# A hybrid decoder layer on one core: the output projection over all 512 tokens of a quarter, norm 2's row scales behind the up projection, and a triangular inverse in place

## The chip, the core and the metric

The kernel runs on one core of a Trainium2 chip. The metric is the device time of one execution in microseconds, the median of several runs; lower is better. The engines are TensorE (PE; PEld is its weight load), VectorE (DVE), ScalarE (ACT), GpSimd (POOL) and SyncE (SP, which issues most of the DMAs).

## The reference

One step of one layer over 2048 prompt tokens and 8 single-token samples, all in float32. Two mixers run side by side on the normed input, a diagonal state space (S5, 512 channels) and a gated delta net (4 heads of 128). Then comes what the change is about:

```python
n = rmsnorm(x, norm1_g); proj = n @ w_in                       # 1024 -> 2568
y_s5 = s5_mixer(...); y_gdn = gdn_mixer(...)                   # chunks of the delta net solve (I + L) X = R, L strictly lower triangular
x = x + concat(y_s5, y_gdn) @ w_out                            # 1024 -> 1024
h = rmsnorm(x, norm2_g) @ w_up                                 # 1024 -> 5632
h = causal_depthwise_conv(h, width 3); gate, up = split(h)
x = x + (silu(gate) * up) @ w_down                             # 2816 -> 1024
y = rmsnorm(x, normf_g)
```

## The kernel before

Activations lie transposed, channels on partitions and tokens in columns. The tokens are worked through in four quarters of 512 (`QT`); the first carries the 8 samples behind its tokens (`NQ` = 520 columns). Each product is made to float32 accuracy out of three matmuls of rounded operands: both sides are split into `hi` and `lo` (`split`: a rounding copy on ACT, a subtraction on DVE or POOL), and `mm3` (L286) adds hi x hi, hi x lo and lo x hi in PSUM. A weight tile is 128 output channels by 1024 inputs. `wsplit` loads it into one of `NWR` = 2 raw buffers `wr` and splits it into `whi` and `wlo`, of which there are four pairs (`NW` = 8). `mm24` (L305) runs its 24 matmuls, 8 input tiles by 3. PSUM tiles hold 512 columns; the tags `mm` (projections) and `d` (down projection) have two each. `blocks(q)` are one block of 512 columns, or 256 and 264 in the first quarter; `halves(q)` are two halves in all quarters.

Program order comes from strings of letters (`FFN`, L44): `r` is the next piece of the generator `rest()`, F, I and B are the front, the inverse and the back of a delta net head, so that a quarter's FFN runs beside the next quarters' heads. A scheduler then sets each engine's order from that and from its estimate of times; what it made of the change is shown further below.

Quarters count from 0 in the code. For a quarter q, `ffn` (L1203) does this:

- `ffn_mix` (L1113, called at the end of the quarter before) loads the mixers' outputs and splits them into `nT`.
- `ffn_out` (L1134) runs over the first half of the tokens, then over the second, each over 8 tiles of `w_out`, which so are loaded and split twice. L1144 adds the product to the residual `xr`, loaded by `ffn_res` for two channel tiles and a half of the tokens, into `x2`. `add_squares` (L1101) sums the squares on ACT and POOL.
- Norm 2: `ffn_scales` (L1150) sums over channels with a matmul with ones and takes the inverse root. `ffn_norm` applies weights and row scales to the first half (L195, then a split, L71 and L72) while the second half's projection runs. For the second half only the channels' weights go into `nT` (L1233, L1234); its row scales `rs` come at L1250.
- Four tiles of w_up (`UPS`) are run ahead, in quarters 1 to 3: their first halves before the second half's norm is done, the second halves after it.
- In a loop over 11 pairs of channel tiles, the up projection leaves PSUM through L1249 (ACT, first half) and L1250 (DVE, second half, times `rs`); then come the convolution (L1251, L1254), the gate and the split into `gt`, and `ffn_down` (L1083) adds w_down's product into `x2` at L1097.
- The last `ffn_down` goes over the halves, with squares (L1105, L1107) and the final weights (L1176) behind each group. `finish` (L1178) takes the root of the squares (a matmul with ones, L1185), transposes `x2` (L1196) and writes the result times the row scale (L1198). Its second half is called as `fin` inside the next quarter's `ffn_out`, after its tile 1.

`gdn_inverse` (L890) makes the inverse of I - L for the four chunks of a head out of `LT`, in the tile `T2T`, of which there are two.

Of the kernel before, what the change touches and what calls it, by code (L numbers as in the profile page):

```python
# [1453 lines left out]
```

## Time and profile before

| | us |
|---|---|
| runs of the kernel | 2874.18, 2874.52, 2877.04 |
| their median | 2874.52 |
| span of the profiled execution, first to last instruction | 2874.3 |
| PE busy in it | 2715.0 (94%) |
| DVE busy | 2176.9 (76%) |
| ACT busy | 1476.0 (51%) |
| POOL busy | 609.6 (21%) |
| HBM read and written | 279.29 MB and 47.29 MB |

The profiled execution's own time is its span, and it stands at the runs' median. Busy is the time in which at least one instruction of the engine runs. Matmuls overlap, so a busy PE isn't yet one at its peak; how close it is shows in the distance between starts. The granted clock is the share of PE's full 2.4 GHz that it was given; half of it is 1.2 GHz.

### The profile page before, as it was taken

What the parts mean: (1) busy time and instruction counts of PE and PEld (TensorE: products, weight loads), DVE (VectorE), ACT (ScalarE), POOL (GpSimd) and SP (SyncE); (2) the same over time, 40 slices, a digit from 0 to 9 for tenths busy, and PEclk for the clock granted to TensorE, in tenths of its full rate; (3) what the DMA queues carried; (4) which work ended last, traced back from release to release, by engine and by line L of the source; (5) the groups of instructions that cost most, each with busy time, mean ns of one, the idle gap of its engine ahead of it and who ended that gap; (6) DMA issues with size and microseconds to landing.
All of it is one profiled execution on the core that took longest, in us unless ns stands there. A gap on an engine that the chain in (4) does not pass through costs nothing.

```text
span 2874.3 us, 45554 instructions
## 1 busy us (share of the span) xinstructions
PE 2715.0 (94%) x16103; PEld 2337.9 (81%) x16103; DVE 2176.9 (76%) x4964; ACT 1476.0 (51%) x3051; POOL 609.6 (21%) x970
## 2 busy tenths in 40 slices
PE   6998788899999999998899999999999998999998
PEld 4798676786888999998887888878888787888887
DVE  8949898856688787778588687887768667676666
ACT  4446565653665554455564554555545445444444
POOL 4325332100121122222221100113211112211112
PEclk9999887898999999999999999999999999999999
DMA  7644433453644232233533333245333334523332
GB/s 205 199 134 132 113 109 92 105 133 104 182 110 117 77 103 87 89 97 111 155 115 109 100 91 98 84 137 174 93 96 97 90 93 144 157 88 96 95 97 74
DMA packets 457657, 329.30 MB, mean 115 GB/s; under 512 B 74960, under 2 KB 412249, under 8 KB 457412
## 3 DMA queue, kind: packets, MB, share of 16 engines
q1 hardware_dynamic: 447091, 297.77, 35.8%
q0 software_dynamic: 10336, 28.61, 3.4%
q8 instruction: 127, 2.08, 0.3%
q14 instruction: 103, 0.84, 0.1%
HBM read 279.29 MB, written 47.29 MB: 114 GB/s over the span
## 4 chain that ended last, share of the span: by engine, by line
PE 66%; DVE 17%; DMA 8%; ACT 4%; issue 3%; POOL 0%; SPq 0%; DVEq 0%; POOLq 0%; ACTq 0%
PE psmm L287 15%; PE psmm L288 15%; PE psmm L289 15%; PE psd L287 5%; PE psd L288 5%; PE psd L289 5%; DVE wlo L72 3%; DVE t L823 1%; ACT whi L71 1%; DVE X L907 1%; DMA xr<-xTD 1%; DMA mr<-mixT 1%; DVE x L1097 1%; DVE hh L649 1%; DMA wr<-in_w_out_dram 1%
## 5 line engine op out<-in xcount | busy, mean ns | idle before, releaser
L287 PE MATMUL psmm<-nT,whi 128*128 128x512 f32 (+2 forms) x3232 | 1115.5, 347 | 45.2 <-ACT whi L71 9.6
L288 PE MATMUL psmm<-nT,whi 128*128 128x512 f32 (+2 forms) x3232 | 1110.3, 344 | 4.8 <-DVE nT L224 3.0
L289 PE MATMUL psmm<-nT,wlo 128*128 128x512 f32 (+2 forms) x3232 | 1107.2, 343 | 1.7 <-POOL wlo L72 1.0
L287 PEld LDWEIGHTS psmm<-nT,whi 128*128 128x128 f32 x3232 | 622.5, 193 | 120.3 <-ACT whi L71 11.7
L288 PEld LDWEIGHTS psmm<-nT,whi 128*128 128x128 f32 x3232 | 624.5, 193 | 73.1 <-DVE nT L224 4.5
L71 ACT ACTIVATE whi<-wr 128x1024 fp32r<-128x1024 f32 x404 | 427.2, 1059 | 496.3 <-PE psmm L288 309.9
L289 PEld LDWEIGHTS psmm<-nT,wlo 128*128 128x128 f32 x3232 | 623.0, 193 | 72.4 <-issue 1.9
L72 DVE TENSOR_TENSOR wlo<-wr,whi 128x1024 fp32r<-128x1024 f32 x388 | 482.3, 1246 | 193.2 <-ACT whi L71 187.4
L1097 DVE TENSOR_TENSOR x<-psd,x 128x512 f32<-128x512 f32 (+2 forms) x464 | 255.6, 558 | 127.3 <-PE psd L289 125.2
L287 PE MATMUL psd<-gt,whi 128*128 128x512 f32 (+2 forms) x928 | 323.6, 350 | 12.7 <-DVE x L1097 10.4
L288 PE MATMUL psd<-gt,whi 128*128 128x512 f32 (+2 forms) x928 | 316.5, 342 | 0.0
L289 PE MATMUL psd<-gt,wlo 128*128 128x512 f32 (+2 forms) x928 | 314.6, 340 | 0.0
L1254 DVE SCALAR_TENSOR_TENSOR t<-raw,cc,t 128x512 f32<-128x512 f32 x352 | 271.5, 772 | 37.1 <-ACT t L1251 27.5
L1255 POOL COPY halo<-raw 128x2 f32<-128x2 f32 x176 | 49.6, 282 | 850.7 <-DVE raw L1250 765.9
L1251 ACT ACTIVATE t<-raw,cc 128x512 f32<-128x512 f32 (+1 forms) x176 | 127.2, 723 | 170.0 <-DVE raw L1250 156.7
L287 PEld LDWEIGHTS psd<-gt,whi 128*128 128x128 f32 x928 | 175.0, 189 | 42.5 <-DVE x L1097 18.8
L72 POOL TENSOR_TENSOR gt<-s,gt 128x512 fp32r<-128x512 f32 (+1 forms) x88 | 134.7, 1531 | 350.4 <-ACT gt L71 341.6
L288 PEld LDWEIGHTS psd<-gt,whi 128*128 128x128 f32 x928 | 175.1, 189 | 20.6
L289 PEld LDWEIGHTS psd<-gt,wlo 128*128 128x128 f32 x928 | 174.9, 189 | 20.8
L1107 POOL TENSOR_TENSOR sq<-sq 128x256 f32<-128x256 f32 (+1 forms) x112 | 109.8, 981 | 219.1 <-ACT sq L1105 213.1
L906 DVE TENSOR_TENSOR tm<-X,N 128x124 f32<-128x124 f32 (+30 forms) x496 | 125.4, 253 | 26.7 <-DMA N<-nD 17.6
L907 DVE TENSOR_TENSOR X<-X,tm 128x124 f32<-128x124 f32 (+30 forms) x496 | 129.6, 261 | 8.4
(503 smaller groups left out, 3666.5 us busy)
## 6 DMA issues: line engine op xcount, KB each, us to landing
wr<-in_ffn_w_up_dram SPq DMA_DIRECT2D x176, 512.0 KB
wr<-in_ffn_w_down_dram SPq DMA_DIRECT2D x88, 512.0 KB
wr<-in_w_in_dram SPq DMA_DIRECT2D x64, 512.0 KB
wr<-in_w_out_dram SPq DMA_DIRECT2D x64, 512.0 KB
xTD<-xT SPq DMA_DIRECT2D x32, 256.0 KB
N<-nD SPq DMA_DIRECT2D x16, 512.0 KB
mr<-mixT SPq DMA_DIRECT2D x32, 256.0 KB
xr<-xTD SPq DMA_DIRECT2D x32, 256.0 KB
```

What stands on the lines that cost most here:

```text
L71: nc.scalar.activation(hi, raw, AF.Copy)
L72: (eng or nc.vector).tensor_tensor(lo, raw, f32(hi), op=OP.subtract)
L287: nc.tensor.matmul(out, lhsT=wh, rhs=xh, start=first, stop=False)
L288: nc.tensor.matmul(out, lhsT=wh, rhs=xl, start=False, stop=False)
L289: nc.tensor.matmul(out, lhsT=wl, rhs=xh, start=False, stop=last)
L906: nc.vector.tensor_tensor(m, X[:, :, j:j + 1].to_broadcast(sh), N[:, j:j + 1, j + 1:].to_broadcast(sh), op=OP.mult)
L907: nc.vector.tensor_tensor(X[:, :, j + 1:], X[:, :, j + 1:], m, op=OP.add)
L1097: nc.vector.tensor_tensor(x2[:, j, b0:b1], p, x2[:, j, b0:b1], op=OP.add)
L1107: c.nc.gpsimd.tensor_tensor(acc[0], acc[0], s, op=OP.add)
L1251: nc.scalar.activation(t[:, :n], raw[:, 2:2 + n], AF.Copy, scale=w[2])
L1254: nc.vector.scalar_tensor_tensor(t[:, :QT], raw[:, j:j + QT], w[j], t[:, :QT], op0=OP.mult, op1=OP.add)
L1255: nc.gpsimd.tensor_copy(c.halo[:, ch], raw[:, QT:QT + 2])
```

## The change

The output projection takes all 512 tokens (520 in the first quarter) per tile of w_out, so each tile is loaded and split once a quarter. In quarters 1 to 3 the first two products are made before `fin` is called and their residuals are added behind it. Only the channels' weights go into `nT` for all columns, in place, tile 0 to 6 behind the matmuls of the last product; norm 2's row scales for all tokens (`rs2`, now 520 columns) are made after the first up tile (`AT`) and multiplied in where the up projection leaves PSUM, on DVE alone. The four up tiles ahead run over 512 columns. The residual comes a channel tile at a time. The inverse is built in `LT` itself; the two `T2T` tiles are gone, and the general pool has 9 buffers for 8 (`NV`).

```diff
-    nc, gp, tt = c.nc, c.gp, c.TT
+    nc, gp, tt, T = c.nc, c.gp, c.TT, LT
...
-def ffn_out(c, q, x2, nT, b0, b1, acc, xrs):
-    nc = c.nc
-    w = b1 - b0
-    for j in range(8):
-        if j % 2 == 0:
-            xr = xrs.pop(0) if xrs else ffn_res(c, q, b0, b1, j)
-        p = c.ps("mm")[:, :w]
-        mm24(c, p, wcols(c, c.w_out, j * 128), nT, b0, b1)
-        nc.vector.tensor_tensor(x2[:, j, b0:b1], p, xr[:, j % 2], op=OP.add)
-        add_squares(c, acc, x2[:, j, b0:b1])
-        yield j
+def ffn_out(c, q, x2, nT, acc, xrs, fin):
+    nc, n = c.nc, ncols(q)
+    def product(j):
+        return j, xrs.pop(0) if xrs else ffn_res(c, q, j), proj(c, q, nT, c.w_out, j * 128)
+    def residual(j, xr, pr):
+        for b0, b1, p in pr:
+            nc.vector.tensor_tensor(x2[:, j, b0:b1], p, xr[:, b0:b1], op=OP.add)
+        add_squares(c, acc, x2[:, j, :n])
+    def columns(kt):
+        g, x, hi, lo = c.col1(C_G2 + kt), x2[:, kt, :n], nT[:, kt, 0, :n], nT[:, kt, 1, :n]
+        nc.scalar.activation(hi, x, AF.Copy, scale=g)
+        nc.vector.scalar_tensor_tensor(lo, x, g, f32(hi), op0=OP.mult, op1=OP.subtract)
+    if q:
+        first = [product(j) for j in (0, 1)]
+        fin()
+        for f in first:
+            residual(*f)
+        yield
+    for j in range(2 if q else 0, 7):
+        residual(*product(j))
+        if j % 2:
+            yield
+    last = product(7)
+    for kt in range(7):
+        columns(kt)
+    residual(*last)
+    columns(7)
...
-def ffn_norm(c, x2, nT, b0, b1, acc):
-    rsB = ffn_scales(c, acc, b1 - b0)
-    for kt in range(8):
-        norm_split(c, nT, kt, x2[:, kt, b0:b1], c.col1(C_G2 + kt), rsB, b0, b1)
-        yield
...
+    yield from ffn_out(c, q, x2, nT, acc, xrs, fin)
     ups = {}
-    if q:
-        for ch in UPS:
-            w, p = wcols(c, c.w_up, ch * 128), c.ps("mm" if len(ups) < 2 else "d")
-            mm24(c, p[:, 0:256], w, nT, *A)
-            ups[ch] = w, p
...
+    for i, ch in enumerate(UPS):
+        if i == AT:
+            rsB = ffn_scales(c, q, acc, fb.tile([128, NQ], F32, name="rs2", bufs=1))
+        if q:
+            ups[ch] = [(0, QT, c.ps("mm" if i < 2 else "d"))]
+            mm24(c, ups[ch][0][2], wcols(c, c.w_up, ch * 128), nT, 0, QT)
...
-                ps = [ups[ch][1]] if ch in ups else [p for _, _, p in proj(c, q, nT, c.w_up, ch * 128)]
-                nc.scalar.activation(raw[:, 2:2 + b0], ps[0][:, :b0], AF.Copy)
-                nc.vector.tensor_tensor(raw[:, 2 + b0:2 + b1], ps[-1][:, -(b1 - b0):], rsB, op=OP.mult)
+                for b0, b1, p in ups.get(ch) or proj(c, q, nT, c.w_up, ch * 128):
+                    nc.vector.tensor_tensor(raw[:, 2 + b0:2 + b1], p, rsB[:, b0:b1], op=OP.mult)
```

The scheduler's order at three places. First PE, where the third quarter ends and the fourth's output projection goes on; before the change (`psd` holds the down projection's groups and the transposes, `psmm` the projections; `x_6015` is `x2`, `nT_6016` is `nT`):

```order
L289 MATMUL psd<-gt,wlo 128x256
L1196 MATMUL psd<-ident,x_6015 128x128 x12
L1185 MATMUL psf<-ones,sq 128x1 x2
L287 MATMUL psmm<-nT_6016,whi 128x256
L288 MATMUL psmm<-nT_6016,whi 128x256
L289 MATMUL psmm<-nT_6016,wlo 128x256
...
L1196 MATMUL psd<-ident,x_6015 128x128 x4
L287 MATMUL psmm<-nT_6016,whi 128x256
L1196 MATMUL psd<-ident,x_6015 128x128 x4
```

and now (`x2` is `x_6011`, the lines are those of the changed file, L1194 for L1185, L1205 for L1196, L285 to L287 for L287 to L289):

```order
L287 MATMUL psd<-gt,wlo 128x256
L1205 MATMUL psd<-ident,x_6011 128x128 x12
L1194 MATMUL psf<-ones,sq 128x1 x2
L1205 MATMUL psd<-ident,x_6011 128x128 x20
L285 MATMUL psmm<-nT_6012,whi 128x512
```

The 20 transposes of the last group of four and of the second half stood between matmuls of the projection, four at a time; now they stand in one piece ahead of it, and the first two products' 48 matmuls stand further up, between the groups of the down projection.

Second, DVE at the end of the fourth quarter's output projection, before (L1144 adds the residual, L195 and the L72 on `nrm` are the first half's norm, L1234 the second half's, L72 on `wr` splits a weight tile):

```order
L1144 TENSOR_TENSOR x_6015<-psmm,xr 128x256
L195 SCALAR_TENSOR_TENSOR nrm<-x_6015,cc,rq 128x256
L72 TENSOR_TENSOR wlo<-wr,whi 128x1024
L1234 SCALAR_TENSOR_TENSOR nT_6016<-x_6015,cc,nT_6016 128x256 x3
L1144 TENSOR_TENSOR x_6015<-psmm,xr 128x256
L1234 SCALAR_TENSOR_TENSOR nT_6016<-x_6015,cc,nT_6016 128x256
L72 TENSOR_TENSOR nT_6016<-nrm,nT_6016 128x256
L1234 SCALAR_TENSOR_TENSOR nT_6016<-x_6015,cc,nT_6016 128x256 x2
L195 SCALAR_TENSOR_TENSOR nrm<-x_6015,cc,rq 128x256 x2
```

and now (L1141 adds the residual, L1147 is the norm, L1172 begins the row scales):

```order
L1141 TENSOR_TENSOR x_6011<-psmm,xr 128x512
L72 TENSOR_TENSOR wlo<-wr,whi 128x1024
L1147 SCALAR_TENSOR_TENSOR nT_6012<-x_6011,cc,nT_6012 128x512 x6
L1141 TENSOR_TENSOR x_6011<-psmm,xr 128x512
L1147 SCALAR_TENSOR_TENSOR nT_6012<-x_6011,cc,nT_6012 128x512
L72 TENSOR_TENSOR wlo<-wr,whi 128x1024
L1147 SCALAR_TENSOR_TENSOR nT_6012<-x_6011,cc,nT_6012 128x512
L1172 TENSOR_SCALAR rq<-psf,epscol 128x512
```

Two chains of norm work over halves have become one over all tokens, with the last residual inside it and the row scales behind it.

Third, DVE inside the first quarter's FFN, before (L1250 is the second block's eviction; the first block's is L1249 on ACT; L906 and L907 are a head's inverse):

```order
L1250 TENSOR_TENSOR raw<-psmm,rs_8677 128x264
L907 TENSOR_TENSOR X<-X,tm 128x4x10
L1097 TENSOR_TENSOR x_6015<-psd,x_6015 128x256
L906 TENSOR_TENSOR tm<-X,N 128x4x9
L1097 TENSOR_TENSOR x_6015<-psd,x_6015 128x256
```

and now (L1238 evicts both blocks):

```order
L1238 TENSOR_TENSOR raw<-psmm,rs_8562 128x264
L1095 TENSOR_TENSOR x_6011<-psd,x_6011 128x256
...
L1095 TENSOR_TENSOR x_6011<-psd,x_6011 128x256
L904 TENSOR_TENSOR tm<-X,N 128x4x10
L1238 TENSOR_TENSOR raw<-psmm,rs_8562 128x256
```

The first block's eviction, ACT's before, stands in DVE's queue between the other work.

## Rows read from the trace of the kernel before

**Rows 1.** The page, part 1 (busy us, share of the span, instructions) and part 4.

```profile
PE 2715.0 (94%) x16103; PEld 2337.9 (81%) x16103; DVE 2176.9 (76%) x4964; ACT 1476.0 (51%) x3051; POOL 609.6 (21%) x970
...
PE 66%; DVE 17%; DMA 8%; ACT 4%; issue 3%; POOL 0%; SPq 0%; DVEq 0%; POOLq 0%; ACTq 0%
```

**Rows 2.** Stretches: length, busy us of PE, PEld, DVE, ACT, POOL, clock, DMA.

```profile
720.00:840.00 120.00, 109.88 (x693) 99.39 (x692) 93.33 (x213) 73.62 (x167) 22.64 (x29) 0.96 0.56 158
840.00:1310.00 470.00, 466.87 (x3678) 445.39 (x3677) 370.64 (x877) 242.69 (x487) 107.65 (x209) 1.00 0.33 93
1310.00:1475.00 165.00, 148.52 (x1089) 136.99 (x1088) 117.80 (x264) 90.54 (x198) 37.74 (x52) 0.96 0.47 137
1475.00:1915.00 440.00, 437.10 (x2125) 350.08 (x2123) 353.55 (x764) 232.14 (x454) 58.11 (x123) 1.00 0.34 99
1915.00:2030.00 115.00, 107.74 (x824) 102.75 (x823) 88.53 (x186) 64.46 (x138) 34.57 (x41) 0.97 0.54 162
2395.00:2505.00 110.00, 95.84 (x698) 90.06 (x697) 76.33 (x135) 52.47 (x96) 35.04 (x38) 0.94 0.53 158
```

**Rows 3.** Timeline of PE: start us, us, instruction, idle us before it and releaser.

```profile
792.67 0.56 PE L287 MATMUL psmm<-nT,whi 128*128 128x264 f32 x1 [5.70 <-ACT ot L958]
1411.24 0.47 PE L287 MATMUL psmm<-nT,whi 128*128 128x512 f32 x1 [3.07 <-ACT whi L71]
2451.27 0.58 PE L287 MATMUL psmm<-nT,whi 128*128 128x256 f32 x1 [3.20 <-DVE x L1144]
2474.56 0.55 PE L287 MATMUL psmm<-nT,whi 128*128 128x256 f32 x1 [3.02 <-ACT whi L71]
```

**Rows 4.** The chain of waits before three of these gaps: start us, us, what.

```profile
784.36 6.82 DMA wr<-in_w_out_dram
...
2444.45 6.33 DMA xr<-xTD
...
2462.06 4.67 DMA wr<-in_w_out_dram
```

**Rows 5.** Groups by line and shape: count | busy us, mean ns | idle before.

```profile
L72 DVE TENSOR_TENSOR wlo<-wr,whi 128x1024 fp32r<-128x1024 f32 x388 | 482.3, 1246 | 193.2 <-ACT whi L71 187.4 <-DMA out_dram<-S0s 1.8 <-PE psd L287 0.9
L71 ACT ACTIVATE whi<-wr 128x1024 fp32r<-128x1024 f32 x404 | 427.2, 1059 | 496.3 <-PE psmm L288 309.9 <-DMA wr<-in_ffn_w_up_dram 58.4 <-DMA wr<-in_w_out_dram 33.4
L1097 DVE TENSOR_TENSOR x<-psd,x 128x512 f32<-128x512 f32 x240 | 163.1, 686 | 95.6 <-PE psd L289 93.8
L1250 DVE TENSOR_TENSOR raw<-psmm,rs 128x256 f32<-128x256 f32 x126 | 52.6, 417 | 0.0
```

**Rows 6.** Timeline of PE behind the gap that ends at 2451.27.

```profile
2451.65 0.42 PE L288 MATMUL psmm<-nT,whi 128*128 128x256 f32 x1
...
2456.78 0.41 PE L288 MATMUL psmm<-nT,whi 128*128 128x256 f32 x1
```

**Rows 7.** Timeline of PE at full clock, pairs in succession.

```profile
2438.36 0.28 PE L289 MATMUL psmm<-nT,wlo 128*128 128x256 f32 x1
2438.47 0.28 PE L287 MATMUL psmm<-nT,whi 128*128 128x256 f32 x1
...
2600.16 0.39 PE L287 MATMUL psd<-gt,whi 128*128 128x512 f32 x1
2600.39 0.39 PE L288 MATMUL psd<-gt,whi 128*128 128x512 f32 x1
```

**Rows 8.** Stretches in which a quarter's last down projection runs.

```profile
1915.00:1954.00 39.00, 35.23 (x243) 30.95 (x241) 37.50 (x83) 24.48 (x54) 13.32 (x17) 1.00 0.47 140
2395.00:2432.00 37.00, 29.52 (x192) 24.68 (x190) 32.75 (x61) 19.11 (x36) 13.33 (x15) 1.00 0.45 141
```

**Rows 9.** Timeline of PE: transposes after the third quarter, and at the kernel's end.

```profile
2428.71 0.66 PE L1196 MATMUL psd<-ident,x 128*128 128x128 f32 x4
...
2432.78 0.39 PE L287 MATMUL psmm<-nT,whi 128*128 128x256 f32 x1
...
2861.51 0.65 PE L1196 MATMUL psd<-ident,x 128*128 128x128 f32 x4 [0.16 <-DVE x L1097]
...
2867.66 1.24 PE L1196 MATMUL psd<-ident,x 128*128 128x128 f32 x8 [1.03 <-ACT yout L1198]
```

More of the change, by code (lines that the diff above doesn't have):

```diff
@@ L23 @@
 NCH = 256
-NW, NWR, NV, NG, NM, UPB = 8, 2, 8, 4, 9, 1
+NW, NWR, NV, NG, NM, UPB = 8, 2, 9, 4, 9, 1
 PB = dict(mm=2, f=2, b=1, i=1)
-UPS = (0, NCT, 1, NCT + 1)
-FIN = 1
 NP = 0
 SMP = 0
+UPS = (0, NCT, 1, NCT + 1)
+AT = 1
 UNQ = (3, 2, 1)
@@ L150, in consts @@
     nc.gpsimd.memset(c.halo, 0.0)
-    c.T2 = [cp.tile([128, 4, 128], F32, name=f"T2T{i}") for i in range(2)]
     c.TT = cp.tile([128, 4, 64], F32, name="TT")
-    for t in (*c.T2, c.TT):
-        nc.gpsimd.memset(t, 0.0)
+    nc.gpsimd.memset(c.TT, 0.0)
     c.Xi = cp.tile([128, 4, 32], F32, name="Xi")
@@ L942, in gdn_inverse, with gdn_back @@
     nc.scalar.activation(T[0:64, :, 64:128], px3[0:64], AF.Copy)
-def gdn_back(c, q, h, col, F, T):
+def gdn_back(c, q, h, col, F):
     nc, gp, sm = c.nc, c.gp, c.sm
     S0 = c.Sst[:, h]
-    kq, kg, vt, AT, hc, zs, _ = F
+    kq, kg, vt, AT, hc, zs, T = F
     ot = gp.tile([128, QT], F32, name="ot", bufs=1).rearrange("p (a b) -> p a b", a=4)
@@ L1120, in ffn_mix @@
         split(nc, nT[:, k, 0, :n], nT[:, k, 1, :n], raw[:, :n])
-    return [ffn_res(c, q, *halves(q)[0], j) for j in (0, 2)]
-def ffn_res(c, q, b0, b1, j):
-    w, e = b1 - b0, min(b1, QT)
-    kp = lambda t: t.rearrange("(k p) t -> p k t", p=128)
-    xr = c.V("xr")[:, :2 * w].rearrange("p (k t) -> p k t", k=2)
-    c.nc.sync.dma_start(xr[:, :, :e - b0], kp(c.xTD)[:, j:j + 2, q * QT + b0:q * QT + e])
-    if b1 > QT:
-        c.nc.sync.dma_start(xr[:, :, e - b0:], kp(c.xTD)[:, j:j + 2, 2048:2056])
-    return xr
@@ L1135, in ffn_out @@
-def ffn_out(c, q, x2, nT, b0, b1, acc, xrs):
-    nc = c.nc
-    w = b1 - b0
-    for j in range(8):
-        if j % 2 == 0:
-            xr = xrs.pop(0) if xrs else ffn_res(c, q, b0, b1, j)
-        p = c.ps("mm")[:, :w]
-        mm24(c, p, wcols(c, c.w_out, j * 128), nT, b0, b1)
-        nc.vector.tensor_tensor(x2[:, j, b0:b1], p, xr[:, j % 2], op=OP.add)
-        add_squares(c, acc, x2[:, j, b0:b1])
-        yield j
-def ffn_scales(c, acc, w, y=None):
-    nc = c.nc
-    a, t = (c.V("rq")[:, :w] for _ in range(2))
-    y = c.V("rq")[:, :w] if y is None else y
-    p = c.ps("f")[:, :w]
-    nc.tensor.matmul(p, lhsT=c.ones, rhs=acc[0], start=True, stop=True)
-    nc.vector.tensor_scalar(a, p, 1.0 / D, c.epscol, op0=OP.mult, op1=OP.add)
-    return rsqrt_(nc, a, y, t)
@@ L1160, in ffn_norm, with ffn_res @@
-def ffn_norm(c, x2, nT, b0, b1, acc):
-    rsB = ffn_scales(c, acc, b1 - b0)
-    for kt in range(8):
-        norm_split(c, nT, kt, x2[:, kt, b0:b1], c.col1(C_G2 + kt), rsB, b0, b1)
-        yield
+    return [ffn_res(c, q, j) for j in (0, 1)]
+def ffn_res(c, q, j):
+    xr = c.V("xr")
+    c.nc.sync.dma_start(xr[:, :QT], c.xTD[j * 128:(j + 1) * 128, q * QT:(q + 1) * QT])
+    if q == 0:
+        c.nc.sync.dma_start(xr[:, QT:NQ], c.xTD[j * 128:(j + 1) * 128, 2048:2056])
+    return xr
+def ffn_out(c, q, x2, nT, acc, xrs, fin):
[25 more added lines that the diff above has]
+    columns(7)
@@ L1168, in ffn_final, with ffn_scales @@
+def ffn_scales(c, q, acc, y):
+    nc = c.nc
+    for b0, b1 in blocks(q):
+        a, t = (c.V("rq")[:, :b1 - b0] for _ in range(2))
+        p = c.ps("f")[:, :b1 - b0]
+        nc.tensor.matmul(p, lhsT=c.ones, rhs=acc[0][:, b0:b1], start=True, stop=True)
+        nc.vector.tensor_scalar(a, p, 1.0 / D, c.epscol, op0=OP.mult, op1=OP.add)
+        rsqrt_(nc, a, y[:, b0:b1], t)
+    return y
 def ffn_final(c, q, x2):
@@ L1207, in ffn @@
     A, B = halves(q)
[L1208 to L1237 removed]
+    acc = []
+    yield from ffn_out(c, q, x2, nT, acc, xrs, fin)
+    ups = {}
+    for i, ch in enumerate(UPS):
[4 more added lines that the diff above has]
+            mm24(c, ups[ch][0][2], wcols(c, c.w_up, ch * 128), nT, 0, QT)
     yield
@@ L1342, in step @@
                 q, h, col, F = st.todo.pop(0)
-                gdn_back(c, q, h, col, F, c.T2[h % 2])
+                gdn_back(c, q, h, col, F)
             elif s == "N":
```

27 lines of the change are left out of this document (2 added, 25 removed).

## The prediction

> **What bounds the kernel now.** (The code counts quarters from 0; first to fourth are its 0 to 3.) I read the page's busy line first: TensorE (PE) is busy for 2715.0 of 2874.3 us, VectorE (DVE) for 2176.9, ScalarE (ACT) for 1476.0 [rows 1]. A share over the whole span says little here, so I cut the FFN part of the span into stretches [rows 2]. Inside a quarter's FFN PE stands idle for 3.1 us in 470 and 2.9 in 440: nothing but PE matters there. Between two quarters, where the output projection and norm 2 lie, it idles 10.1 of 120 us, 16.5 of 165, 7.3 of 115 and 14.2 of 110, together 48.1 us, and there its granted clock is 0.96, 0.96, 0.97 and 0.94 of full, where the FFN stretches show 1.00. One minus the clock, times the length, is 4.8 + 6.6 + 3.5 + 6.6 = 21.5 us at most. So about 70 us lie in the four transitions, and a change of the projection and of norm 2 can win no more than that plus what PE's own work shrinks.
>
> Then I looked for what ends PE's idle time there. Four of the longest rows are 5.70, 3.07, 3.20 and 3.02 us [rows 3]. The chain of waits names what came last before them [rows 4]: a load of a tile of w_out (6.82 us), a residual load (6.33 us, queued behind weight loads), and not long before the fourth another load of w_out (4.67 us), between the whi (1.06 us) and wlo (1.25 us) of other tiles [rows 5]. That loop explains the stretch. There are two raw weight buffers, and one is free again when whi and wlo are made of it, so a tile takes (4.67 + 1.06 + 1.25) / 2 = 3.5 us at least while the loads take that long. PE asks for a tile every 24 x 0.12 = 2.9 us when the tile meets 256 columns. It starves by some 0.6 us a tile, and the start of the stage, where several loads crowd, makes long gaps of it.
>
> After such a gap PE runs slowly: behind the one of 3.20 us 25 matmuls of 256 columns follow each other, the first at 2451.65, the last at 2456.78, 0.21 us apart [rows 6], where 0.12 is the pace at full clock [rows 7]: 25 x 0.09 = 2.3, with the first one 2.5 us more.
>
> **The change part by part.**
>
> Fewer, longer matmuls. In quarters 1 to 3, 8 tiles of w_out and 4 of w_up go from two matmuls of 256 columns to one of 512: 3 x 12 x 24 = 864 pairs. At full clock a row of 256 is followed after 0.11 to 0.12 us, one of 512 after 0.23 [rows 7], so the pair costs what the long one costs, to 0.01 us: I take 864 x 0.003 = 2.6 us won (9 lost to 9 won).
>
> Half the w_out tiles. 32 loads of 512 KB go, with 32 whi on ACT (1.06 us) and 32 wlo on DVE (1.25 us) [rows 5]. Those engines had slack there, so their 34 and 40 us aren't the gain. The gain is that a tile now feeds 24 x 0.233 = 5.6 us of PE against the loop's 3.5 us: the starvation ends. I credit the four long gaps, 15.0 us, with a slow stretch of 2.5 us behind each: 25 us. Upper bound: all 70 us; lower bound: 9 us, the two gaps (5.70 and 3.20) whose chain leads to w_out's own queue, without the slow stretches.
>
> More to do while the last down projection runs. That part, done in two halves with squares and scaling, is bound by DVE: 37.50 us busy of 39 at the third quarter's start, 32.75 of 37 at the fourth's [rows 8], while PE idles 3.8 and 7.5 us. The two products whose PSUM is free then are now 11.2 us of PE instead of 5.7. In the order of the third and fourth quarters they stand between the down projection's groups, in the second they come mostly after it. I take 3 us in two quarters, 6 in all (0 to 11).
>
> A wait that is new: the residual of channel tile 0 is now written over all 512 tokens, so it must follow the transposes of the last quarter's second half, and product 2 needs its PSUM. Now these transposes stand singly between matmuls; in the changed order all 20 stand in one piece, right before product 2. The kernel's own end has the same order without cover and prices it [rows 9]: from the first transpose (2861.51) to the end of the last (2868.90) 7.4 us. Of these 32 x 0.11 = 3.5 us are work that stays. Today the first 12 transposes and what follows take 4.1 us (2428.71 to 2432.78), and 20 more between matmuls some 2.2 to 2.8 us: 6.6. So 0.8 us is lost, and a slow stretch of 2.5 us comes with it, and the residual itself 0.69 us: 4 us in each of two quarters, 8 in all (2 to 13). The second quarter has 43 of the 48 matmuls behind the transposes as cover.
>
> Norm 2. Before, the first half's columns took two DVE operations and a copy each; now all take one copy and one DVE operation over 512 columns, in place, each behind the last product's matmul that reads it. Eight at about 0.75 us are 6 us beside 5.6 us of product 7 and 22 us of the four up tiles that follow; the row scales (five DVE and two ACT operations of some 0.7 us, 5 us) are asked for only by the eviction of the first up tile, 17 us of matmuls later. I cost it at 0. If the cover were gone it would be 5 us a quarter, 20 us. In quarter 0, which has no up tiles ahead, the projections of the next delta net head stand there in the order: 42 + 54 matmuls of 512 columns, 22 us.
>
> Evictions of the up projection. Today ACT takes 256 columns and DVE the rest (0.417 us); now DVE takes all, in quarters 1 to 3 as one of 512 (0.686 us, by the down projection's addition of the same shape) [rows 5]. DVE gains 132 x 0.27 = 36 us and in quarter 0, with its two blocks, 44 x 0.42 = 18 us. Inside the FFN that makes DVE 353.6 + 12 of 440 us busy in the second quarter and 370.6 + 18 of 470 in the first [rows 2], 83% each. In quarter 0 a block of matmuls lasts 24 x 0.12 = 2.9 us and two blocks of PSUM are all there is, and every block must now come through DVE's queue, behind a wlo of 1.25 us, say. I take 3 us there, 0 elsewhere (0 to 37, below).
>
> The inverse in place of L^T. No instruction goes but two memsets on POOL; L^T's buffer is held until the head's back part, as A^T's already is, and the front of the next head but one comes after that in the order. 0, and the room goes to a ninth buffer of the general pool. The stretch before 720 us is only reordered by the scheduler: 0, give or take 5 us, which no row prices.
>
> Sum: 25 + 6 + 2.6 - 8 - 3 = 23 us, from 2874.3 us of the profiled execution to **2851 us**. The median of the runs, 2874.52, is the same within 0.01%.
>
> **Rivals.**
>
> Larger gain: the transitions close nearly, 40 to 55 us won, 2819 to 2836 us. For it: 70 us are idle or slow. Against it: the DVE-bound end of each quarter and the transposes stay. 8%.
>
> The waits move: the starvation ends, but norm 2's chain, the transposes and the residual now lie in one line per quarter. If each of four quarters loses 5 us at the row scales, the 23 us are gone: 2866 to 2880 us. For it: all tokens now wait at one point, where before one half covered the other. Against it: 17 us of cover. 16%.
>
> DVE becomes the bound inside the FFN: slower. In quarter 0 there are 88 blocks; if each waits 0.42 us for the eviction that ACT used to make beside it, 37 us are lost, and the time is 2874 - 26 + 37 = 2885 us. It decides from 0.3 us a block on. For it: DVE already has 17% of the chain [rows 1]. Against it: PE idles only 3.1 us in that stretch with DVE 79% busy, and ACT had to wait for PE there as well. The Trainium skill (Perfetto Trace Analysis, Optimizing Scalar/DVE Operations) speaks for this rival: where DVE is saturated, it says, moving some work to ScalarE may help, and the change does the reverse. By that rule the trace agrees only in so far as DVE is near 80% there. 14%.
>
> That the change doesn't do what it says can be left out: the order has 32 loads of w_out fewer.
>
> **How the numbers follow.** The forecast, 2836 to 2866 us, has 62%. A measurement of this kernel tells some 0.2%, 5.7 us, from no change: faster is below 2868.8 us, slower above 2880.3. Faster: 62 + 8 and a fifth of the 16, 73%. Same: the rest of those, 13%. Slower: 14%. The range 2822 to 2876 leaves out some 2% below and 18% above.
>
> **What would show it.** Right: PE's idle time between quarters down by 15 to 25 us with no gap of 3 us behind a whi or a w_out load; the granted clock there up; the FFN stretches as long as now. Transposes: a stretch of 7 us before the third product in the last two quarters, with a clock below full behind it. Wrong: PE idle behind the multiplication by the row scales inside quarter 0, or behind the row scales' chain; or a stretch before 720 us that has moved by more than 5 us.

## The result, and the profile after

The changed kernel takes 2849.03 us (median of 4 runs, 2843.12 to 2856.1), the kernel before in the same comparison 2875.78. The ratio is 0.9907, 95% interval 0.989 to 0.9923: faster by 27 us (22 to 32). The forecast was 2851. The profiled execution, with a span of 2841.3 us, is the quickest of the four; it lies 33.0 us under the span of before, so its stages sum to more than the medians differ.

The page of the changed kernel, part 1 and part 4, against [rows 1]:

```profile
PE 2696.8 (95%) x15233; PEld 2278.9 (80%) x15233; DVE 2151.1 (76%) x4873; ACT 1383.6 (49%) x2773; POOL 668.5 (24%) x940
...
PE 72%; DVE 16%; DMA 5%; issue 3%; ACT 3%; SPq 0%; POOL 0%; POOLq 0%; DVEq 0%; ACTq 0%
```

PE was busy 18.2 us less and yet has 72% of the chain instead of 66; DMA's share fell from 8 to 5%. The stretches that answer to [rows 2], columns as there (the cuts follow the same stages):

```profile
720.00:831.00 111.00, 103.64 (x681) 92.75 (x680) 83.45 (x189) 60.58 (x132) 17.53 (x20) 0.97 0.45 124
831.00:1308.00 477.00, 472.61 (x3697) 451.47 (x3696) 381.97 (x917) 232.46 (x455) 106.04 (x211) 1.00 0.33 93
1308.00:1462.00 154.00, 144.75 (x808) 120.79 (x806) 103.77 (x227) 78.63 (x170) 35.83 (x42) 0.98 0.43 126
1462.00:1894.00 432.00, 426.84 (x2062) 341.84 (x2063) 358.44 (x764) 219.34 (x409) 82.76 (x125) 1.00 0.34 97
1894.00:2002.00 108.00, 103.50 (x544) 85.21 (x543) 71.85 (x135) 50.70 (x97) 31.61 (x33) 0.98 0.45 135
2369.00:2471.00 102.00, 93.85 (x455) 75.47 (x454) 67.31 (x111) 47.28 (x82) 32.02 (x33) 0.98 0.46 142
```

PE's idle time in the four transitions is 7.4 + 9.3 + 4.5 + 8.2 = 29.3 us, where it was 48.1. One minus the clock, times the length, is 3.3 + 3.1 + 2.2 + 2.0 = 10.6 us, where it was 21.5.

Cuts at round times don't hold the same work, so I also measured between events: a stage "FFN" runs from the first to the last addition of the down projection in a quarter (L1097 before, L1095 after), a stage "between" from that last one to the first of the next quarter. From the starts of these additions in the traces, in us:

```
                 start   FFN1  betw.1-2  FFN2  betw.2-3  FFN3  betw.3-4  FFN4
before           888.4  473.3    136.7  452.4    101.7  376.9    100.8  331.9
changed          886.8  476.4    128.6  448.8     95.2  377.7     89.2  326.4
changed-before    -1.6    3.1     -8.1   -3.6     -6.5    0.8    -11.6   -5.5
load_twice       892.1  478.9    132.8  451.1     96.3  381.5     91.3  326.4
split_twice      884.8  476.8    131.2  448.9     95.6  376.5     92.8  326.0
no_filler        886.1  466.1    140.5  441.0    104.1  371.6    102.6  326.4
spare_psum       883.6  476.9    128.5  449.2     97.5  386.4     79.9  326.7
at3              891.9  477.2    132.5  454.8     99.2  373.9     91.5  326.0
e_act_q0         890.7  480.1    128.5  449.1     96.3  377.7     89.2  326.4
t2t_after        892.9  476.5    132.3  456.4     95.4  374.4     90.7  326.5
inplace_before   886.4  474.3    148.4  446.7    106.6  377.6     98.2  331.8
inplace_nv8      898.6  475.8    137.3  450.8     99.5  378.0    101.0  331.7
nwr3_before      891.3  473.0    146.6  447.3     99.3  375.7    103.6  331.4
w_out_twice      893.6  476.6    134.1  450.4     99.8  378.0     97.1  326.0
short_mm         893.2  476.4    127.5  452.8     96.4  379.5     90.1  326.7
```

Of 33 us, 26.2 came out of the three stages between quarters, 5.5 out of the fourth FFN. That one is no faster: the trace of before has 22 more 512-column matmuls in it (886 for 864; 22 x 0.23 = 5.1 us), which the change put ahead of its first addition. The first quarter's projection lies in "start" and won next to nothing. Each row is one execution, and its sums are good to some us only: short_mm, whose runs are no longer than the changed kernel's (below), is 7.1 us longer from the first FFN on.

In the last transition the chain of waits of the changed kernel has no load from the first product after the transposes on (start us, us, what):

```profile
2388.91 4.79 DMA mixT<-zs
2393.77 2.85 DMA mr<-mixT
...
2420.28 1.24 PE psd L1205 x8
2421.52 0.38 PE psmm L285
...
2463.50 0.86 PE psf L1171 x2
```

Between the last two lines, 42 us, every piece of the chain is a matmul of PE: the loads of w_out and of the residuals, which stood there in [rows 4], are hidden. In the two transitions before it the chain has none of them either (1375 to 1462 and 1940 to 2002 us). Only the last down projection still has two transfers in the chain, the store and the load of a head's output (`mixT`).

### The profile page after: what moved, and what is told of

Same layout as the page of the kernel before. It is cut to its first block, busy times and chain, and to the rows that moved or that the text cites. A ratio compares the mean times of both kernels' runs of the same rounds, so it can differ in the third digit from the quotient of the medians.

```text
span 2841.3 us, 43162 instructions
## 1 busy us (share of the span) xinstructions
PE 2696.8 (95%) x15233; PEld 2278.9 (80%) x15233; DVE 2151.1 (76%) x4873; ACT 1383.6 (49%) x2773; POOL 668.5 (24%) x940
## 4 chain that ended last, share of the span: by engine, by line
PE 72%; DVE 16%; DMA 5%; issue 3%; ACT 3%; SPq 0%; POOL 0%; POOLq 0%; DVEq 0%; ACTq 0%
PE psmm L285 16%; PE psmm L286 16%; PE psmm L287 16%; PE psd L285 5%; PE psd L286 5%; PE psd L287 5%; DVE wlo L72 2%; DVE X L905 1%; DVE x L1095 1%; DVE tm L904 1%; DVE hh L647 1%; DVE t L821 1%; DVE nT L72 1%; DMA N<-nD 1%; DVE t L1242 1%
## 5 line engine op out<-in xcount | busy, mean ns | idle before, releaser
L285 PE MATMUL psmm<-nT,whi 128*128 128x512 f32 (+2 forms) x2992 | 1068.8, 359 | 21.3 <-ACT t L818 5.0
L286 PE MATMUL psmm<-nT,whi 128*128 128x512 f32 (+2 forms) x2992 | 1062.5, 355 | 4.7 <-DVE nT L222 3.2
L287 PE MATMUL psmm<-nT,wlo 128*128 128x512 f32 (+2 forms) x2992 | 1060.1, 355 | 1.0 <-POOL wlo L72 0.9
L71 ACT ACTIVATE whi<-wr 128x1024 fp32r<-128x1024 f32 x372 | 393.5, 1059 | 649.7 <-PE psmm L286 468.2
L285 PEld LDWEIGHTS psmm<-nT,whi 128*128 128x128 f32 x2992 | 570.4, 191 | 104.9 <-ACT t L818 7.2
L286 PEld LDWEIGHTS psmm<-nT,whi 128*128 128x128 f32 x2992 | 572.0, 191 | 83.2 <-DVE nT L222 4.8
L287 PEld LDWEIGHTS psmm<-nT,wlo 128*128 128x128 f32 x2992 | 571.1, 191 | 81.5 <-issue 2.3
L72 DVE TENSOR_TENSOR wlo<-wr,whi 128x1024 fp32r<-128x1024 f32 x356 | 439.3, 1235 | 99.6 <-ACT whi L71 94.7
L1095 DVE TENSOR_TENSOR x<-psd,x 128x512 f32<-128x512 f32 (+2 forms) x464 | 256.7, 557 | 154.3 <-PE psd L287 152.6
L285 PE MATMUL psd<-gt,whi 128*128 128x512 f32 (+2 forms) x928 | 323.7, 349 | 15.3 <-DVE x L1095 14.8
L287 PE MATMUL psd<-gt,wlo 128*128 128x512 f32 (+2 forms) x928 | 315.9, 342 | 0.0
L1242 DVE SCALAR_TENSOR_TENSOR t<-raw,cc,t 128x512 f32<-128x512 f32 x352 | 278.1, 792 | 15.7 <-ACT t L1239 11.2
L1243 POOL COPY halo<-raw 128x2 f32<-128x2 f32 x176 | 72.0, 409 | 803.1 <-DVE raw L1238 723.3
L285 PEld LDWEIGHTS psd<-gt,whi 128*128 128x128 f32 x928 | 175.4, 189 | 45.6 <-DVE x L1095 22.7
L72 POOL TENSOR_TENSOR gt<-s,gt 128x512 fp32r<-128x512 f32 (+1 forms) x88 | 130.2, 1479 | 334.0 <-ACT gt L71 333.9
L287 PEld LDWEIGHTS psd<-gt,wlo 128*128 128x128 f32 x928 | 175.3, 189 | 21.0
L1238 DVE TENSOR_TENSOR raw<-psmm,rs 128x512 f32<-128x512 f32 (+1 forms) x214 | 123.7, 578 | 69.1 <-PE psmm L287 67.6
L1105 POOL TENSOR_TENSOR sq<-sq 128x256 f32<-128x256 f32 (+3 forms) x84 | 96.4, 1148 | 207.3 <-ACT sq L1103 204.4
```

Of the source, the lines that this page charges most:

```text
L285: nc.tensor.matmul(out, lhsT=wh, rhs=xh, start=first, stop=False)
L286: nc.tensor.matmul(out, lhsT=wh, rhs=xl, start=False, stop=False)
L287: nc.tensor.matmul(out, lhsT=wl, rhs=xh, start=False, stop=last)
L1095: nc.vector.tensor_tensor(x2[:, j, b0:b1], p, x2[:, j, b0:b1], op=OP.add)
L1105: c.nc.gpsimd.tensor_tensor(acc[0], acc[0], s, op=OP.add)
L1238: nc.vector.tensor_tensor(raw[:, 2 + b0:2 + b1], p, rsB[:, b0:b1], op=OP.mult)
```

## The experiments

Intervals are those of the ratio to the kernel before, measured on the same chip. "Over the changed kernel" is the difference of the two ratios times 2876 us; by the roots of the summed squares of the intervals' halves it is good to some 6 us. So only differences of 8 us and more stand on the ratio alone; of smaller ones the stages speak. The scheduler orders each variant anew, too: 814 of PE's 15233 matmuls stand at another place than in the changed kernel in load_twice, 1663 in split_twice, 2190 in no_filler, 1426 in at3 and 2361 in e_act_q0, so no run changes one thing alone.

**w_out_twice.** Loads and splits of w_out doubled.

```diff
-        return j, xrs.pop(0) if xrs else ffn_res(c, q, j), proj(c, q, nT, c.w_out, j * 128)
...
+        p = c.ps("mm")
+        for k0 in (0, 4):
+            wh, wl = wcols(c, c.w_out, j * 128)
+            for kt in range(k0, k0 + 4):
+                mm3(nc, p, wh[:, kt], wl[:, kt], nT[:, kt, 0, :QT], nT[:, kt, 1, :QT], kt == 0, kt == 7)
+        return j, xr, [(0, QT, p)]
```

> The changed kernel, but in the second to fourth quarter each tile of w_out is loaded and split twice, once for its first four input tiles and once for the last four; the matmuls keep their 512 columns and their order. Starvation theory (the gain came from the raw buffers' loop, 3.5 us a tile): a tile is asked for every 2.8 us again, so most of the 25 us credited to it come back: 2864 to 2874 us, ratio 0.995 to 1.000, with gaps of 2 us and more on TensorE behind whi or a load of w_out between the quarters. Rival (the gain came from the longer matmuls and from more work beside the down projection; the loads were hidden): 2845 to 2854 us, ratio 0.989 to 0.993, no such gap.

Measured 2866.68 us, ratio 0.996 (0.9948 to 0.9973): 15 us over the changed kernel, as the starvation theory had it. But its gaps are not behind w_out: the longest, 7.15 us at 1476.59, is behind an eviction by the row scales. So this doesn't yet say whether transfers or splits cost it. The next two take them apart.

**load_twice** and **split_twice.**

```diff
...
+        if q:
+            c.nc.sync.dma_start(c.WR("wr").rearrange("p (k f) -> p k f", k=8),
+                                c.w_out.rearrange("(k p) f -> p k f", p=128)[:, :, j * 128:j * 128 + 128])
+        return j, xr, proj(c, q, nT, c.w_out, j * 128)
```

```diff
...
+        nc.sync.dma_start(v(wr), c.w_out.rearrange("(k p) f -> p k f", p=128)[:, :, j * 128:j * 128 + 128])
+        for k0 in (0, 4):
+            wh, wl = c.W("whi"), c.W("wlo")
+            split(nc, wh, wl, wr, c.wl)
+            for kt in range(k0, k0 + 4):
+                mm3(nc, p, v(wh)[:, kt], v(wl)[:, kt], nT[:, kt, 0, :QT], nT[:, kt, 1, :QT], kt == 0, kt == 7)
...
```

> The changed kernel with every tile of w_out in the second to fourth quarter loaded a second time into a raw buffer that nobody reads; it is split once. With the twice split twin it takes apart the kernel that did both and came out at ratio 0.996. Starvation theory (loads and raw buffers set the pace): most of that loss, 10 to 18 us over the changed kernel, 2859 to 2867 us, ratio 0.994 to 0.997. Rival (the work of splitting on ScalarE and VectorE sets it): at most 4 us over the changed kernel, ratio 0.990 to 0.992.

> The changed kernel with every tile of w_out in the second to fourth quarter loaded once but split twice, into two pairs of buffers, the first for four input tiles and the second for the other four: 24 more roundings on ScalarE (25 us) and 24 more subtractions on VectorE (30 us). Starvation theory: at most 4 us over the changed kernel, ratio 0.990 to 0.992. Rival (the splits stand in VectorE's and ScalarE's queues ahead of norm 2's columns and of the residuals): 10 to 18 us over it, ratio 0.994 to 0.997, with TensorE waiting for the columns or for the row scales.

Measured: load_twice 2858.94 us, ratio 0.9945 (0.9932 to 0.9957), 11 us over the changed kernel; split_twice 2849.15, ratio 0.9913 (0.9898 to 0.9928), 2 us. The loads cost more than the 55 us of splitting; whether the splits cost nothing can't be told. In the stages from the end of the first FFN on, load_twice is 13.5 us over the changed kernel, split_twice 5.1, which is no more than one execution can show, and w_out_twice, which does both, 19.5. The rival's wait does show in split_twice, once, at the second quarter's first eviction, as in w_out_twice:

```profile
1465.09 0.76 PE L285 MATMUL psmm<-nT,whi 128*128 128x512 f32 x1 [7.19 <-DVE raw L1249]
```

In the changed kernel this wait is 1.01 us. Where the loads cost is told by the chain of load_twice in the last transition:

```profile
2381.77 4.18 DMA wr<-in_w_out_dram
2385.97 0.38 SPq L301
2386.46 4.39 DMA mr<-mixT
...
2396.06 4.38 DMA mr<-mixT
...
2405.76 4.76 DMA mixT<-zs
2410.53 6.09 DMA mr<-mixT
```

and by SP's timeline, the queue that issues them (L1139 is the added load, L301 the one that is used, L1115 loads the mixers' outputs):

```profile
2405.09 0.38 SPq L1139 DMA_DIRECT2D wr<-in_w_out_dram  x1
...
2407.22 0.38 SPq L301 DMA_DIRECT2D wr<-in_w_out_dram  x1
2409.78 0.38 SPq L1139 DMA_DIRECT2D wr<-in_w_out_dram  x1
2410.53 0.45 SPq L1115 DMA_DIRECT2D mr<-mixT  x1
```

The first of the three pieces of the mixers' outputs stands in SP's queue behind a load of w_out, which had to wait until the added load had landed. The last piece is issued when the store that it reads has landed (2405.76 + 4.76); there it is the transfer that is long, 6.09 us where the changed kernel's chain has 2.85, with three weight loads issued in the 5.6 us before it instead of two. So the price of weight loads falls on what stands behind them, by waiting in the queue and by slower transfers; what each is worth isn't shown.

**nwr3_before.** The other side of the same question: the kernel before with a third raw buffer.

```diff
-NW, NWR, NV, NG, NM, UPB = 8, 2, 8, 4, 9, 1
+NW, NWR, NV, NG, NM, UPB = 8, 3, 8, 4, 9, 1
...
-    nc, gp, tt = c.nc, c.gp, c.TT
+    nc, gp, tt, T = c.nc, c.gp, c.TT, LT
```

> The kernel before with a third raw weight buffer, in the room that the inverse in place leaves; projection in halves, norm and evictions as before. Starvation theory: the loop falls to (4.67 + 1.06 + 1.25) / 3 = 2.3 us a tile, below the 2.9 us that TensorE asks for, so the four long gaps between the quarters go: 2848 to 2860 us, ratio 0.991 to 0.996. Rival (the loads are late for another reason, the transfers' own rate or the order of SP's queue): 2870 to 2880 us, ratio 0.998 to 1.002.

Measured 2877.65 us, ratio 1.0 (0.9987 to 1.0012): the starvation theory as predicted is missed. Against inplace_nv8, the same kernel with two raw buffers, it is 7 us faster, not 15 to 25, and in the profiled executions the three transitions are not shorter at all (349.5 us for 337.8). The groups of DVE in the last transition (2437 to 2510 us) show what happened (count | busy, mean ns | idle before and releasers):

```profile
L72 DVE TENSOR_TENSOR wlo<-wr,whi 128x1024 fp32r<-128x1024 f32 x16 | 21.0, 1310 | 2.1 <-ACT whi L71 2.0
L1142 DVE TENSOR_TENSOR x<-psmm,xr 128x256 f32<-128x256 f32 x16 | 6.6, 421 | 21.1 <-PE psmm L287 16.6 <-DMA xr<-xTD 4.0 <-PE psd L1194 0.4
```

VectorE's wait before the splits is nearly gone, 2.1 us; in the kernel before the same group had 12.7 us in its transition (2432 to 2505). But the chain of waits now runs through the residual's loads:

```profile
2450.37 1.24 DVE wlo L72
2451.62 0.38 SPq L301
2452.19 5.30 DMA xr<-xTD
...
2459.64 4.43 DMA xr<-xTD
...
2472.93 1.14 DVE wlo L72
2474.09 0.37 SPq L301
2474.51 5.82 DMA xr<-xTD
```

Each is issued right behind a weight load (L301), and before two of them the chain shows what that load waited for: the split (L72) that frees a raw buffer, with three buffers too. The wait has moved from one load to the other in the same queue. The queue's order isn't all of it, though. The DMA engines (second number from the right: their busy share) are half idle in the kernel before until the buffer is free, and full while the residual of 6.33 us [rows 4] is on its way:

```profile
2436.00:2444.00 8.00, 8.00 (x69) 8.00 (x68) 3.21 (x4) 5.04 (x8) 2.69 (x5) 0.96 0.57 176
2444.00:2451.00 7.00, 4.08 (x35) 3.87 (x34) 1.43 (x3) 3.20 (x5) 3.27 (x4) 0.95 1.00 304
```

So late issue and full DMA engines come together in that wait, and no run takes them apart.

**short_mm.**

```diff
-            mm24(c, ups[ch][0][2], wcols(c, c.w_up, ch * 128), nT, 0, QT)
+            w = wcols(c, c.w_up, ch * 128)
+            for b0, b1 in halves(q):
+                mm24(c, ups[ch][0][2][:, b0:b1], w, nT, b0, b1)
```

and the same in `product`.

> The changed kernel with every 512-column matmul of w_out and of the four up tiles ahead, in the second to fourth quarter, as two of 256, one run of 24 over each half; weights are loaded and split once as now. Prediction's term: 864 pairs at 0.003 us, up to 0.005, are 3 to 4 us: 2851 to 2854 us, ratio 0.991 to 0.993. Rival (the length of the matmuls is the gain): 20 us and more back, 2869 us and more, ratio 0.997 to 1.000.

Measured 2850.58 us, ratio 0.9907 (0.9886 to 0.9929): no difference that the runs tell. PE is busy 2700.9 us for 2696.8, 4.1 more for 864 pairs. The rival, 20 us and more, is out.

**no_filler.**

```diff
...
+        w, p = wcols(c, c.w_out, j * 128), c.ps("mm")
+        nc.vector.tensor_copy(p[:, 0:1], x2[:, 7, QT - 1:QT])
+        mm24(c, p, w, nT, 0, QT)
...
```

> The changed kernel, but in the second to fourth quarter the first two products of the output projection must wait for the end of the last down projection (VectorE first copies one value of the residual's last tile into their PSUM); in the order they then stand between the transposes. Prediction's terms: 11.2 us of matmuls no longer fill the down projection, TensorE idles there as much as before the change or more (4 to 8 us and up to 11), so 6 us are lost, up to 11 a quarter; the transposes are covered again, 2 to 8 us won in all. Together 2845 to 2857 us. Rival (the filler is worth its whole length, because VectorE and not TensorE sets the down projection's time): 20 to 30 us lost, 2869 to 2879 us, ratio 0.997 to 1.001.

Measured 2859.23 us, ratio 0.9934 (0.9918 to 0.995): 8 us over the changed kernel. The end of its third down projection:

```profile
2370.00:2410.00 40.00, 30.00 (x164) 24.93 (x162) 32.74 (x68) 19.44 (x41) 12.55 (x15) 0.91 0.41 127
```

PE idles 10 us of 40 and its granted clock is 0.91; in the changed kernel it idles 5.0 us of the 42 from 2371 to 2413, at 0.96. By the stages, each FFN taken with the transition behind it, the products' place beside the down projection is worth 1.6, 1.1 and 7.3 us in the second, third and fourth quarter, not their length of 11.2. These are net figures: the kernel covers the transposes again, and takes away all 11.2 us, where before the change 5.7 stood there.

**spare_psum.**

```diff
...
+        if q < 3 or j not in (2, 3):
+            return j, xr, proj(c, q, nT, c.w_out, j * 128)
+        w, p = wcols(c, c.w_out, j * 128), c.ps("bi"[j - 2])
+        mm24(c, p, w, nT, 0, QT)
...
```

> The changed kernel, but in the fourth quarter products 2 and 3 of the output projection get the two PSUM banks that the delta net's heads have left free, so they need not wait for the residuals of products 0 and 1 behind the transposes. Prediction's terms: 4 us a quarter for the transposes in one piece and what is left idle in that quarter's last down projection (about 4 us) can be won: 2843 to 2846 us, ratio 0.988 to 0.990. Rival (the transposes are no cost on the path, VectorE's chain through the residuals is): within 1.5 us of the changed kernel.

Measured 2844.34 us, ratio 0.989 (0.9872 to 0.9908), not to be told from the changed kernel. The median lies in the band of the prediction's terms, but the error of some 6 us leaves both sides open. The stages say that nothing was won: FFN3 and the transition behind it take 386.4 + 79.9 = 466.3 us, for 377.7 + 89.2 = 466.9. The work went forward, the end stayed.

**at3.**

```diff
-AT = 1
+AT = 3
```

> The changed kernel with norm 2's row scales asked for after three of the four up tiles ahead instead of after one, so that some 6 us of matmuls cover their chain of 5 us instead of 17. Prediction's term (row scales hidden): 0 to 3 us more, 2848 to 2853 us, ratio 0.990 to 0.993. Rival (the chain was at the edge of its cover already): 5 us a quarter, 10 to 20 us more, 2860 to 2870 us, with TensorE idle behind the multiplication by the row scales at the start of each quarter's FFN.

Measured 2857.24 us, ratio 0.9928 (0.9912 to 0.9943), 6 us over the changed kernel; the three transitions are 3.9, 4.0 and 2.3 us longer. PE at the second quarter's first eviction:

```profile
1471.28 0.77 PE L285 MATMUL psmm<-nT,whi 128*128 128x512 f32 x1 [2.60 <-DVE raw L1238]
```

The same wait is 0.70 us in the third quarter and 0.17 in the fourth, so it doesn't account for all that the transitions lost. In the changed kernel it is 1.01 us, in the second quarter only. So the wait is real, and 17 us of matmuls ahead of it hide nearly all of it; the price of 6 us is within the error.

**e_act_q0.**

```diff
-                    nc.vector.tensor_tensor(raw[:, 2 + b0:2 + b1], p, rsB[:, b0:b1], op=OP.mult)
+                    if q == 0 and b0 == 0:
+                        nc.scalar.activation(raw[:, 2 + b0:2 + b1], p, AF.Copy, scale=rsB[:, 0:1])
+                    else:
+                        nc.vector.tensor_tensor(raw[:, 2 + b0:2 + b1], p, rsB[:, b0:b1], op=OP.mult)
```

> The changed kernel, but in the first quarter the first block's 256 columns leave PSUM through ScalarE, as before the change, multiplied by the first token's row scale alone (so each token's own scale is left out for them). Prediction's term for the evictions on VectorE: 3 us, so 2843 to 2849 us, ratio 0.989 to 0.991, with the first quarter's FFN up to 4 us shorter. Rival (VectorE is the bound there at 0.2 us a block or more): 18 us and more shorter, 2831 us or less, ratio 0.985 or less. Second rival (ScalarE is no better than VectorE there): no change or longer.

Measured 2853.56 us, ratio 0.9925 (0.9908 to 0.9942): 5 us over the changed kernel, within the error. The first quarter's FFN stage of this kernel, which answers to 476.40 us in the changed one with PE busy 467.74 and DVE 385.47:

```profile
890.70:1370.80 480.10, 469.94 (x3602) 443.58 (x3600) 376.76 (x883) 246.51 (x493) 105.00 (x196) 0.99 0.33 95
```

DVE has 9 us less to do, and PE idles 10.2 us instead of 8.7. The second rival holds, no gain. Why the stage is longer is another matter: its longest idle, 2.33 us at 1328.95, is behind a step of a head's inverse on ACT (L922), not behind an eviction. In the changed kernel PE waits for the evictions 0.3 us in this whole stage, and for VectorE's additions of the down projection (L1095) 6.5.

**inplace_before**, **inplace_nv8** and **t2t_after.** The first two are the edit of nwr3_before with `NWR, NV` of 2, 9 and 2, 8. The third undoes it in the changed kernel:

```diff
-NW, NWR, NV, NG, NM, UPB = 8, 2, 9, 4, 9, 1
+NW, NWR, NV, NG, NM, UPB = 8, 2, 8, 4, 9, 1
...
-    nc, gp, tt, T = c.nc, c.gp, c.TT, LT
+    nc, gp = c.nc, c.gp
...
+    tt = gp.tile([128, 1024], F32, name="N", bufs=1)[:, 0:256].rearrange("p (a b) -> p a b", a=4)
+    nc.gpsimd.memset(tt[0:32, :, 32:64], 0.0)
```

> The kernel before with only the inverse in place and the ninth general buffer. Prediction's term: nothing, 2870 to 2880 us, ratio 0.998 to 1.002, and the FFN begins within 5 us of where it did. Rival (the ninth buffer, which loads and norms share, gives part of the gain): 2860 to 2868 us, ratio 0.995 to 0.998.

> The kernel before with the inverse in place and eight general buffers as before; its twin with nine came out 0.46% slower than the kernel before. If the place of the inverse costs that: ratio 1.003 to 1.006, and the stretch between the first and second quarter 8 to 12 us longer than before. If the ninth buffer (other loads ahead of others) does: ratio 0.998 to 1.002.

> The changed kernel with the inverse in tiles of its own again and eight general buffers; for room its small transposed blocks lie in the inverse's input tile, with one more memset on POOL a head. If the inverse in place costs the changed kernel what its twin of the kernel before lost: 8 to 13 us faster than the changed kernel, 2836 to 2841 us, ratio 0.986 to 0.988. Prediction's term (it costs nothing): ratio 0.990 to 0.992.

Measured: inplace_before 2887.34 us, ratio 1.0046 (1.003 to 1.0062); inplace_nv8 2882.98, 1.0025 (1.0014 to 1.0036); t2t_after 2860.09, 0.9947 (0.9934 to 0.9961). In the kernel before, the edit costs 7 us with eight buffers and 13 with nine; undoing it in the changed kernel costs 11 as well. None of the three came out as either side had it, and no price for the edit fits all. By the stages it lands in other places each time: 11.7 us in the first transition (inplace_before), 10.2 us ahead of the first FFN (inplace_nv8), 6.1 there and 7.6 in the second quarter's FFN (t2t_after), all stretches in which heads of the delta net run. The two "ahead" are not the chip's start, since PE's 1500th matmul starts at 281.7 us against 281.6 before, and at 283.8 against 283.7 in the changed kernel; but from there to the first addition kernels with the changed one's order spread over 4.2 us already (602.6 to 606.8), so little stands of the 6.1. That the edit makes the scheduler order the work anew can be read from the traces: PE's matmuls of inplace_before and of the kernel before part at the 64th, those of inplace_nv8 and inplace_before at the 1720th. Whether that order, the number of buffers, or in t2t_after the shared tile costs the time stays open.

## Why the prediction was right, term by term

The forecast, 2851, is 2 us from the median, and the case it named, transitions that shrink, is the one that came. Its terms were not all right, and that it came so near is in part luck: 8.2 us credited to the first quarter did not come, the transposes cost less than the 8 us set against the gain, and the inverse's term can't be told.

**Half the w_out tiles, 25 us.** The size was near, the mechanism half wrong. With 24 of the 32 loads back, 11 to 15 us are gone (load_twice, w_out_twice); the prediction's share for those three quarters was 25 - 5.7 - 2.5 = 16.8. The step that failed is "that loop explains the stretch", (4.67 + 1.06 + 1.25) / 2 with the raw buffers as the limit. A third buffer ended the wait of the splits and not the starvation, and doubled splits cost 2 us by the medians and 5.1 by the stages, where doubled loads cost 11 and 13.5. What the chains show is the loads in SP's queue: weights wait for buffers there, residuals and mixers' outputs stand behind the weights, and the DMA engines are full while they come. [rows 4] had shown it, the residual load of 6.33 us "queued behind weight loads", and the working counted it as w_out's own.

**The first quarter's share, 8.2 us, did not come.** The gap of 5.70 us [rows 3] is gone, and another stands in the same projection, in PE's timeline of the changed kernel:

```profile
807.93 0.40 PE L287 MATMUL psmm<-nT,wlo 128*128 128x512 f32 x1
813.24 0.63 PE L921 MATMUL psi<-TT,LT 32*32 32x32 f32 x8 [4.91 <-DVE TT L911]
```

A head's inverse now ends here, and in DVE's queue its small steps stand between the eight column operations of norm 2 and the splits:

```profile
799.17 0.17 DVE L904 TENSOR_TENSOR tm<-X,N 128x20 f32<-128x20 f32 x1
799.26 1.42 DVE L1147 SCALAR_TENSOR_TENSOR nT<-x,cc,nT 128x520 fp32r<-128x520 f32 x2
800.60 1.30 DVE L905 TENSOR_TENSOR X<-X,tm 128x20 f32<-128x20 f32 x1
801.83 1.42 DVE L1147 SCALAR_TENSOR_TENSOR nT<-x,cc,nT 128x520 fp32r<-128x520 f32 x2
```

The step at 800.60 lasts 1.30 us where its neighbour lasts 0.17. The inverse's result then goes through DRAM, as the chain shows:

```profile
807.35 3.94 DMA xD<-X
811.31 1.55 DMA LT<-xD
```

PE, in whose order the merge's matmuls come next, waits for all of it, and behind the wait runs at half its clock: its matmuls of 512 columns follow 0.43 us apart from 814.39 to 817.80 (granted clock 0.50), where 0.23 is the pace at full clock. The inverse in place isn't the reason, since t2t_after has the same wait (5.47 us at 820.74). This is the rival "the waits move", in one quarter and at another engine's work than it named.

**More beside the last down projection, 6 us.** The sign is right, 8 us are lost without it, but nearly all in the fourth quarter, and no run isolates the step from 5.7 to 11.2 us. **Longer matmuls, 2.6 us.** Right: 4.1 us of PE's busy time, too little for the medians to tell.

**The transposes in one piece, 8 us lost.** The stretch is there, its price only in part. PE's timeline ahead of the fourth quarter's third product:

```profile
2413.09 0.66 PE L1205 MATMUL psd<-ident,x 128*128 128x128 f32 x4
...
2420.28 1.24 PE L1205 MATMUL psd<-ident,x 128*128 128x128 f32 x8 [1.26 <-ACT yout L1207]
2421.40 0.50 PE L285 MATMUL psmm<-nT,whi 128*128 128x512 f32 x1
2421.74 0.39 PE L286 MATMUL psmm<-nT,whi 128*128 128x512 f32 x1
2421.97 0.39 PE L287 MATMUL psmm<-nT,wlo 128*128 128x512 f32 x1
```

8.4 us from the first to the end of the last, where 7.4 was worked out from [rows 9]. But the slow stretch behind it, 2.5 us of the 4, doesn't come: the next matmuls follow at 0.23 us. And to give PE other work there won nothing (spare_psum). Ahead of the third quarter's third product the stretch is longer, 10.1 us, and the clock does fall, inside it:

```profile
1940.41 1.33 PE L1205 MATMUL psd<-ident,x 128*128 128x128 f32 x8
1944.06 0.77 PE L1194 MATMUL psf<-ones,sq 128*128 128x1 f32 x4 [2.32 <-POOL sq L1105]
1944.69 3.56 PE L1205 MATMUL psd<-ident,x 128*128 128x128 f32 x16
1949.26 1.23 PE L1205 MATMUL psd<-ident,x 128*128 128x128 f32 x8 [1.00 <-ACT yout L1207]
```

16 in 3.56 us are 0.22 apiece, twice the 0.11 of full clock. Against the prediction's 6.6 us this quarter loses 3.5, about the 4 forecast, the fourth 1.8; no run gave PE other work in the third.

**Evictions on DVE, 3 us lost.** The stage is 3.1 us longer, and for another reason: it has more work in it, 336 matmuls of 512 columns for 288 before and 50 fewer of 256, and PE idles no more than before (8.7 us for 9.5), 0.3 of it behind evictions. The rival of a DVE-bound FFN is out, with DVE busy 385.47 of 476.4 us. The Trainium skill (Perfetto Trace Analysis, Optimizing Scalar/DVE Operations) says that moving work to ScalarE may help where VectorE is saturated; at 81% busy, moving the first block's evictions there won nothing (e_act_q0).

**Norm 2's row scales, nothing.** Right with the cover there is, to the 1.01 us of the second quarter. There the operations on DVE take 7.7 us (1454.27 to 1461.98) instead of the 5 us of the working, and the same wait is 2.60 us with less cover (at3) and 7.19 us with more splits (split_twice).

**The inverse in place, nothing.** Wrong: in the kernel before the edit costs 7 to 13 us, in the changed kernel undoing it, with the ninth buffer, costs 11. The step that failed is that the 0 was read from the instructions that go (two memsets), where the order of PE's work moves as well. Part of the 27 us may be this term's; how much can't be told from these runs, since the edit's price depends on the rest.

## What to carry to other kernels

When a load is late, ask what stands ahead of it in its queue before counting buffers: here a third buffer moved the wait to the next load in the queue, and halving the weight loads took both out of the chain between the quarters. Work beside a stage that another engine bounds is worth at most what the bounded stage leaves idle, 1 to 7 us of 11.2 here, and not its length. Where a scheduler orders everything, an edit that costs nothing by itself can still move some 10 us either way; run it alone and with the rest before giving it a sign.
